# A layer norm's weights applied before the transpose, and products placed later by a planner

## The chip, the cores and the metric

The kernel runs on one core of a Trainium2 chip. The metric is the device time of one execution in microseconds (us). The engines of the core are TensorE (PE, matrix products; PEld is its loading of the stationary operand), VectorE (DVE), ScalarE (ACT), GpSimd (POOL) and SyncE (SP, which here issues nearly all transfers). They run side by side, each in the order in which its instructions were written, and wait for each other by semaphores.

## The reference

Two layers over 256 rows of 1,024 channels, then one more norm. A layer normalises its input, multiplies it by 9,808 columns of weights at once, lets three kinds of attention work on parts of the product, gates and merges their outputs, and adds the result to the input:

```
h = rms_norm(x, gain)                          # x * rsqrt(mean(x*x) + eps) * gain
proj = einsum('bsd,de->bse', h, w_in)
oa = moba_attention(rope(qa), rope(ka), va) * silu(ga)
ob = dsa_attention(rope(qb), rope(kb), vb, q_idx, k_idx, w_idx) * silu(gb)
log_f = log_sigmoid(f_logit + f_bias)
oc = forgetting_attention(qc, kc, vc, log_f) * silu(gc)    # logits + cumulative sums of log_f
y = einsum('nbsw,nwd->bsnd', stack([oa, ob, oc]), w_branch)
merged = sum(sigmoid(merge_logit) * y, over the three)
x = x + einsum('bsd,de->bse', merged, w_out)
```

After the second layer the rows are normalised with final_gain. Each attention has 8 heads of 64 columns.

## The kernel before

**Products in two parts.** All large products are made from float32 values split in two: a high part in the type fp32r and a low part, the rest. A weight comes from memory into one of three buffers called raw (1 MB each); ACT copies it into the high part wh (L381) and DVE subtracts to get the low part wl (L385). PE then adds three products: high by high, low by high and high by low. The normalised rows stand transposed as hTh and hTl. The sums grow in three banks called proj; d (two tiles of two banks) takes scores and transposes, and o (one bank) the attention's output.

**The order of work.** The program does not write its instructions as it states them. Each operation is put down with the tokens that it reads and writes, an estimated cost and a key (`plan.op`, L120). Then `Plan.run` (L150) goes through time: among the operations whose operands are there, it takes the engine that can start first, and on it the operation of the lowest key among those that can start then. The order that comes out is written to the engines, SP's queue of transfers included. An operation may carry a margin: the planner takes its operands to be there that much later than estimated. The estimate has no part in the run itself; where an operand comes later than planned, the engine waits with all that it has queued.

**Units.** A unit is one block of columns: `unit_a` (rows by 512 columns of weights, stationary the rows), `unit_b` (256 columns of weights stationary in two halves). Units are numbered as they are stated, and the number is the key of its matmuls; weight splits have a key 2 lower, their transfers 12 lower. A layer states, in this order, the first values (va), the index keys (kwf), the index scores and the MoBA mixer "a" mixed with gate units (m), the values and the mixer of "c" (forgetting attention), those of "b" (DSA), the rest of m and y, and the output product o.

**The norm** (`norm_to_hT`, L523) is made twice per layer, for each tile t of 128 rows: sums of squares of the two halves of 512 columns (L499 on ACT, L501 on DVE; in the second layer ACT alone), the mean (L505, DVE), the power -0.5 (L507, POOL), the rows times this factor (`scaled`: half 0 on ACT, L516, half 1 on DVE, L519), then eight transposes of 128 x 128 on PE (L537), and for each of the eight blocks a copy times the weight of the channel into hTh (L544, ACT) and a subtraction into hTl (L551, DVE). After the transpose a channel is a partition, so its weight is one scalar per partition, from the tile gT, which the host lays out as columns.

**The forget sums** (`wf_cols`, L783) make the forget gate's logarithms and their cumulative sums right after the index keys: exponential and logarithm on ACT (L802, L803; the logarithm needs another function table), nine small operations on DVE (L808 to L816), three products (L822 to L824), a transpose, and a way through memory into brow, which mixer c's biases read (L672).

**Attention** goes by pairs of heads: scores on PE (L613), maximum on DVE (L687), exponential on ACT (L691), normalising, transposes of the probabilities on PE (L624), split into pth (L716, ACT) and ptl (L717, DVE), and the values' products on PE (L729 to L732), of which L731 and L732 read ptl. Scores, transposes and values' products carry a margin of 200 ns (MARGIN).

**The opening.** SP sends the two halves of the first rows, the first weights, gT, and so on. PE runs 14 products of ones (L955) while nothing is there yet, and ten more (L1035, "warm") are planned at the lowest priority. `first_v` makes va of layer 0 in finer pieces: 48 matmuls of 512 columns (L1027).

**The last layer's end** sends final_gain, spread over the partitions, to acc (L1102) once the merged rows in acc have been read by the transposes L941; the output product adds to x (L1114), and the final norm follows.

Of the kernel before, what the change touches and what calls it, by code (L numbers as in the profile page):

```python
# [9 lines left out]
F32 = mybir.dt.float32  # L10
# [35 lines left out]
O_ORDER = ((0, (0, 1)), (1, (0, 1)), (0, (2, 3)), (1, (2, 3)))  # L46
M_ORDER = ((0, (0, 1)), (1, (0, 1)), (0, (2, 3)), (1, (2, 3)))
# [58 lines left out]
class Op:  # L106
    __slots__ = ("ways", "deps", "bufs", "new", "key", "n", "out", "need", "eng", "end", "lag", "name", "start",
                 "margin", "port", "banks")


class Plan:
# [8 lines left out]
    def op(self, ways, reads, writes, key, lag=0.0, name="", touch=()):  # L120
        o = Op()
        o.ways, o.key, o.lag, o.name, o.margin, o.port = ways, key, lag, name, 0.0, False
# [27 lines left out]
    def run(self, slack):  # L150
# [4 lines left out]
        while ready:  # L155
# [36 lines left out]
            e = min(best, key=best.get)  # L192
            lim = best[e] + slack.get(e, 0.0)
            t, _, _, o, w = min((c for c in cand if c[4][0] == e and c[0] <= lim), key=lambda c: (c[1], c[2]))
# [54 lines left out]
def hybrid_trunk(ctx, tc, x, norm_gain, w_in, forget_bias, w_branch, w_out, final_gain, consts, out):  # L249
# [51 lines left out]
    gT = pool.tile([128, L, KC], F32, name="gT")  # L301
# [29 lines left out]
    k_id, k_rope, k_gT, k_cst, k_fb, k_wf, k_widx, k_lf, k_cs, k_csT, k_main = (Tok() for _ in range(11))  # L331
# [179 lines left out]
    def scaled(i, src, t, reads, key):  # L511

        r = small[:, t, 3:4]
        o = tmp6[:, i * HD:(i + 1) * HD]
        if i == 0:
            act(lambda: ACT.activation(o, src, AF.Copy, scale=r), HD, False, reads + [k_ss[t][2]], [k_tmp[i]], key,  # L516
                "norm", 93.0)
        else:
            dve(lambda: DVE.tensor_scalar(o, src, r, None, op0=ALU.mult), HD, reads + [k_ss[t][2]], [k_tmp[i]], key,  # L519
                "norm", t_dve2(HD) + 61.0)  # L520
        return o

    def norm_to_hT(l, t, key):  # L523
        for i in range(2):
            sum_sq(t, i, key, l == 0)
        rstd(t, key)
        for i in range(2):
            scaled(i, xs[t][:, i * HD:(i + 1) * HD], t, [k_x[t][i]], key)
        dd = [Buf("d"), Buf("d")]
        for b in range(4):  # L530
            ps, at = Tok(), [dd[b // 2], dd[b // 2].banks[b % 2]]
            at_cols = lambda k, d=dd[b // 2], b=b: T(d)[:, b % 2 * 512 + k * 128:b % 2 * 512 + (k + 1) * 128]

            def tr(b=b, at_cols=at_cols):
                for k in range(2):
                    c = b * 2 + k
                    PE.transpose(at_cols(k), tmp6[:, c * 128:(c + 1) * 128], ident)  # L537
            pe(tr, 220.0, [k_tmp[b // 2], k_id], [ps], key, "hT", touch=at)
            for k in range(2):
                c = b * 2 + k  # L540
                sl = (slice(None), c, slice(t * 128, (t + 1) * 128))
                src = lambda at_cols=at_cols, k=k: at_cols(k)
                g = gT[:, l, c:c + 1]
                act(lambda sl=sl, src=src, g=g: ACT.activation(hTh[sl], src(), AF.Copy, scale=g), 128, True,  # L544
                    [ps, k_gT], [k_hT[0][t][c]], key, "hT", 93.0, touch=at)
            for k in range(2):
                c = b * 2 + k
                sl = (slice(None), c, slice(t * 128, (t + 1) * 128))
                src = lambda at_cols=at_cols, k=k: at_cols(k)
                g = gT[:, l, c:c + 1]  # L550
                dve(lambda sl=sl, src=src, g=g: DVE.scalar_tensor_tensor(  # L551
                    hTl[sl], src(), g, hTh[sl].bitcast(F32), op0=ALU.mult, op1=ALU.subtract), 128,
                    [ps, k_gT, k_hT[0][t][c]], [k_hT[1][t][c]], key, "hT", t_dve(128) + 61.0, touch=at)
# [520 lines left out]
    for l in range(L):  # L1074
# [15 lines left out]
        for f in between(first, m_of(l, 0, gates) + m_of(l, 2, gates, HC)):  # L1090
            f()
# [57 lines left out]
```

## Time and profile before

| What | Value |
|---|---|
| Median of 3 runs | 599.27 us (599.0 to 599.41) |
| The profiled execution | 598.98 us |
| Its span, first to last instruction | 597.1 us |
| TensorE's granted clock, mean | 0.999 |
| POOL busy | 100.2 us, 110 instructions |
| Bytes moved | 107.59 MB, mean 180 GB/s |

The profile is of one execution. A row of the timeline has the start and the duration in us, the engine, the line of the kernel, the operation, the tiles written and read, the shapes, how many like it follow each other, and, in brackets, how long the engine was idle before it and what ended that. Matmuls overlap, and their ends are modelled: a row of many shows a pitch, not a duration of one. The loading of a stationary operand (PEld) stands in rows of its own and runs ahead of the matmul. A row of waits has the total, the number and the longest. SP's waits are those of its queue of transfers.

### The profile page before, as it was taken

To read this page: it belongs to the slowest core of one execution; us is meant where nothing else is said; L and a number is where in the kernel's file an instruction comes from. 1 tells how busy PE (TensorE), PEld (TensorE's weight loads), DVE (VectorE), ACT (ScalarE), POOL (GpSimd) and SP (SyncE) were. 2 spreads that over 40 slices of the span, in tenths; PEclk is the share of its full clock that TensorE was granted. 3 is DMA by queue.
4 is the path that set the end of the run, shared out by engine and by line. 5 is a ranking of instruction groups with operands and counts; after the bars stand their busy time and mean duration, and the time that the engine had idled before them with its cause. 6 is when DMAs were issued, how large, how long until landed. Compare 5 with 4: busy or idle time off the path is not lost.

```text
span 597.1 us, 11359 instructions
## 1 busy us (share of the span) xinstructions
PE 587.2 (98%) x4332; PEld 538.2 (90%) x4332; DVE 516.8 (87%) x1164; ACT 387.0 (65%) x736; POOL 100.2 (17%) x110
## 2 busy tenths in 40 slices
PE   8999999999999999999999999999999999999995
PEld 7989998989998999888889899898999899998885
DVE  6799999877898989978588999997869898998773
ACT  5767539585677757774487754676748785758441
POOL 1241040200000334200004221320000023440001
PEclk9999999999999999999999999999999999999999
DMA  8849546546464554474546747464574464447411
GB/s 289 278 145 349 176 131 228 181 136 213 140 212 143 155 199 142 145 264 155 164 141 212 249 149 240 142 212 143 176 246 143 141 212 142 143 144 271 150 35 72
DMA packets 75831, 107.59 MB, mean 180 GB/s; under 512 B 4208, under 2 KB 45440, under 8 KB 75776
## 3 DMA queue, kind: packets, MB, share of 16 engines
q1 hardware_dynamic: 75488, 106.47, 54.4%
q8 instruction: 34, 0.56, 0.4%
q10 hardware_dynamic: 288, 0.39, 0.2%
q14 instruction: 21, 0.17, 0.1%
HBM read 105.79 MB, written 1.06 MB: 179 GB/s over the span
## 4 chain that ended last, share of the span: by engine, by line
PE 85%; DVE 10%; issue 2%; ACT 1%; DMA 1%; POOL 0%; POOLq 0%; DVEq 0%
PE proj L429 74%; PE d L613 4%; DVE wl L385 3%; PE proj L1027 2%; PE d L624 2%; PE o L732 1%; PE o L729 1%; DVE isc L891 1%; DVE t L890 1%; PE o L731 1%; PE d L941 1%; DVE rsh L488 1%; DMA x<-in_x_dram 1%; PE o L730 0%; ACT wh L381 0%
## 5 line engine op out<-in xcount | busy, mean ns | idle before, releaser
L385 DVE TENSOR_TENSOR wl<-raw,wh 128x1024 fp32r<-128x1024 f32 (+1 forms) x190 | 235.1, 1250 | 26.3 <-ACT wh L381 23.2
L381 ACT ACTIVATE wh<-raw 128x1024 fp32r<-128x1024 f32 (+1 forms) x190 | 198.2, 1055 | 74.7 <-PE proj L429 37.1
L429 PE MATMUL proj<-hTh,wh 128*128 128x256 f32 (+1 forms) x656 | 155.6, 276 | 0.0
L429 PE MATMUL proj<-hTl,wh 128*128 128x256 f32 (+1 forms) x656 | 154.9, 275 | 0.0
L429 PEld LDWEIGHTS proj<-hTh,wh 128*128 128x128 f32 (+1 forms) x656 | 125.2, 191 | 0.6
L429 PEld LDWEIGHTS proj<-hTl,wh 128*128 128x128 f32 (+1 forms) x656 | 125.2, 191 | 0.3
L429 PE MATMUL proj<-wh,hTh 128*128 128x512 f32 x272 | 105.1, 386 | 0.0
L429 PE MATMUL proj<-wh,hTl 128*128 128x512 f32 x272 | 103.3, 380 | 0.2 <-DVE hTl L551 0.2
L429 PE MATMUL proj<-hTh,wl 128*128 128x256 f32 (+1 forms) x656 | 100.4, 276 | 0.0
L429 PEld LDWEIGHTS proj<-hTh,wl 128*128 128x128 f32 (+1 forms) x656 | 86.2, 191 | 0.2
L429 PE MATMUL proj<-wl,hTh 128*128 128x512 f32 x272 | 81.0, 379 | 0.3 <-DVE wl L385 0.3
L489 POOL TENSOR_TENSOR rsh<-rsh,cst 128x256 f32<-128x256 f32 (+1 forms) x42 | 38.4, 915 | 165.9 <-DVE rsh L488 164.3
L429 PEld LDWEIGHTS proj<-wl,hTh 128*128 128x128 f32 x272 | 51.3, 189 | 7.9 <-DVE wl L385 0.7
L429 PEld LDWEIGHTS proj<-wh,hTl 128*128 128x128 f32 x272 | 51.5, 189 | 7.5 <-DVE hTl L551 1.2
L429 PEld LDWEIGHTS proj<-wh,hTh 128*128 128x128 f32 x272 | 51.4, 189 | 7.5
L691 ACT ACTIVATE e<-e,st 128x128 f32<-128x128 f32 x96 | 42.4, 443 | 22.8 <-DVE st L687 22.5
L491 POOL TENSOR_TENSOR rr<-rr,rsh 128x256 f32<-128x256 f32 (+1 forms) x42 | 41.5, 989 | 12.6 <-DVE rr L490 8.8
L752 POOL TENSOR_TENSOR ot<-ot,g 128x256 f32<-128x256 f32 x10 | 8.1, 814 | 200.6 <-DVE ot L747 129.1
L429 PE MATMUL proj<-wh,v 128*128 128x512 f32 (+1 forms) x144 | 34.0, 359 | 0.0
L429 PEld LDWEIGHTS proj<-wh,v 128*128 128x128 f32 x144 | 25.1, 190 | 2.8
L429 PE MATMUL proj<-wh,og0h 128*128 128x512 f32 x64 | 25.0, 391 | 0.0
L717 DVE TENSOR_TENSOR ptl<-d,pth 128x768 fp32r<-128x768 f32 x24 | 22.9, 953 | 2.2 <-ACT pth L716 1.9
(193 smaller groups left out, 926.8 us busy)
## 6 DMA issues: line engine op xcount, KB each, us to landing
raw<-in_w_in_dram SPq DMA_DIRECT2D x74, 1024.0 KB, 5.2
raw<-in_w_branch_dram SPq DMA_DIRECT2D x12, 1024.0 KB, 5.1
raw<-in_w_out_dram SPq DMA_DIRECT2D x8, 1024.0 KB, 5.1
brow<-drow SPq DMA_DIRECT2D x4, 512.0 KB, 6.6
raw<-in_w_in_dram SPq DMA_DIRECT2D x3, 512.0 KB, 6.2
x<-in_x_dram SPq DMA_DIRECT2D x4, 256.0 KB, 5.5
raw<-in_w_in_dram SPq DMA_DIRECT2D x2, 320.0 KB, 6.2
out_dram<-tmp SPq DMA_DIRECT2D x2, 320.0 KB, 2.5
```

The lines of the kernel that those rows point to most:

```text
L381: ACT.activation(p[0].v, sel(c.v), AF.Copy)
L385: DVE.tensor_tensor(p[1].v, sel(c.v), p[0].v.bitcast(F32), op=ALU.subtract)
L429: PE.matmul(o(), a(), b(), start=first and i == 0, stop=last and i == n - 1)
L488: dve(lambda: DVE.stream_shuffle(T(sh)[:np_], a(), SWAP), S, [ps], [sh], key, "rope", t_dve(S) + 6.0)
L489: gps(lambda: POOL.tensor_tensor(T(sh)[:np_], T(sh)[:np_], s[:np_], op=ALU.mult), S, [k_rope], [sh], key, "rope")
L491: gps(lambda: POOL.tensor_tensor(T(r)[:np_], T(r)[:np_], T(sh)[:np_], op=ALU.add), S, [sh], [r], key, "rope")
L613: PE.matmul(T(d)[:, c:c + n].rearrange("p (b a) -> p b a", a=2), st[r, sl], turns(mv[r, :n]), start=i == 0, stop=i == 2, skip_group_check= ...
L624: PE.matmul(T(d)[:, u * 512 + j * 64:u * 512 + j * 64 + 64], e[r], ident[r, r], is_transpose=True, start=True, stop=True, skip_group_check ...
L691: act(lambda t=t, a=a, n=n, e=e, st=st: ACT.activation(T(e)[:, a:a + n], T(e)[:, a:a + n], AF.Exp, bias=T(st)[:, t:t + 1], scale=-1.0, acc ...
L717: dve(lambda src=src, dst=dst: DVE.tensor_tensor(dst(pl), src(), dst(ph).bitcast(F32), op=ALU.subtract), 128 * n, [ps, k[0]], k[1:], key, ...
L752: plan.op([("POOL", t_pool(S), lambda: POOL.tensor_tensor(*gate(), op=ALU.mult)), ("DVE", t_dve(S), lambda: DVE.tensor_tensor(*gate(), op= ...
L1027: PE.matmul(T(ps[t]).rearrange("p (b a) -> p b a", a=2), h(2 * i + x, t), turns(v3(w)[:, x]), start=left[t][0] == 23, stop=left[t][0] == 0)
```

## The change

- **The norm.** The weights multiply the rows before the transpose, where a channel is a column. So they are needed as a row, the same on all partitions. For layer 0 the row (4 KB) is the first transfer of all, into a part of brow; two products of a single row of ones with 512 columns of it spread it over the partitions into a tile of d (gain0, held until both tiles of rows have been normed). For layer 1 the row is sent spread to acc, as the final gain was, before the output product's units of layer 0. One DVE instruction per half (rows times factor times weights) takes the place of `scaled`. gT and the host's layout for it go.
- **512 wide.** Per half: four transposes, one copy to hTh, one subtraction to hTl (before: eight blocks of 128, two by two). A tile of rows uses one tile of d instead of two. Sums of squares may go to either engine in both layers.
- **Rush.** Operations of the norm that only DVE or POOL can do may be taken up to 400 ns ahead of their start by the planner, so that the engine is kept for them. In layer 1 the norm's keys are the unit's less 10 and 8 (before: less 2).
- **Margins.** Scores and transposes of the probabilities 300 ns, values' products 600 ns (before: 200 for all).
- **The forget sums** get the key of the unit after mixer a instead of the index keys'; only the part that reads the product's result from the bank stays.
- **The opening.** Each tile of rows is one transfer, not two halves; the memset of half comes after the first loads; one early Tanh on ACT.

```diff
+RUSH = 400.0
+NK = (10, 8)
...
-            e = min(best, key=best.get)
+            e = min(cand, key=lambda c: c[0] - c[3].rush)[4][0]
             lim = best[e] + slack.get(e, 0.0)
-            t, _, _, o, w = min((c for c in cand if c[4][0] == e and c[0] <= lim), key=lambda c: (c[1], c[2]))
+            t, _, _, o, w = min((c for c in cand if c[4][0] == e and c[0] <= lim + c[3].rush), key=lambda c: (c[1], c[2]))
...
     def norm_to_hT(l, t, key):
+        a = len(plan.ops)
         for i in range(2):
-            sum_sq(t, i, key, l == 0)
-        rstd(t, key)
+            sum_sq(t, i, key, True)
+        r = rstd(t, key)
+        d = Buf("d")
         for i in range(2):
...
+            c = slice(i * HD, (i + 1) * HD)
+            x, o = xs[t][:, c], tmp6[:, c]
+            g = (lambda c=c: T(gain0)[:, c]) if l == 0 else (lambda c=c: acc[:, 0, c])
+            rg, tg = ([k_gain], [gain0]) if l == 0 else ([k_fg, k_acc[0][0], k_acc[1][0]], [])
+            dve(lambda x=x, o=o, g=g: DVE.scalar_tensor_tensor(o, x, r, g(), op0=ALU.mult, op1=ALU.mult), HD,
+                [k_x[t][i], k_ss[t][2]] + rg, [k_tmp[i]], key, "norm", touch=tg)
+            at, kt, ks4 = [d, d.banks[i]], Tok(), slice(4 * i, 4 * i + 4)
+
+            def tr(i=i, o=o, d=d):
+                for j in range(4):
+                    PE.transpose(T(d)[:, i * 512 + j * 128:i * 512 + (j + 1) * 128], o[:, j * 128:(j + 1) * 128], ident)
+            pe(tr, 480.0, [k_tmp[i], k_id], [kt], key, "hT", touch=at)
+            src = lambda i=i, d=d: T(d)[:, i * 512:(i + 1) * 512].rearrange("p (k s) -> p k s", k=4)
+            h, lo = (x[:, ks4, t * 128:(t + 1) * 128] for x in (hTh, hTl))
+            act(lambda h=h, src=src: ACT.activation(h, src(), AF.Copy), HD, True, [kt], k_hT[0][t][ks4], key, "hT", touch=at)
+            dve(lambda h=h, lo=lo, src=src: DVE.tensor_tensor(lo, src(), h.bitcast(F32), op=ALU.subtract), HD,
+                [kt] + k_hT[0][t][ks4], k_hT[1][t][ks4], key, "hT", t_dve(HD) + 10.0, touch=at)
+        for o in plan.ops[a:]:
+            if {w[0] for w in o.ways} <= {"DVE", "POOL"}:
+                o.rush = RUSH
...
-        pe(go, sum(cost) + SWITCH, [r for x in reads for r in x], [w for x in writes for w in x], key, name, MARGIN,
+        pe(go, sum(cost) + SWITCH, [r for x in reads for r in x], [w for x in writes for w in x], key, name, 300.0,
...
-            pe(av, 696.0, kv + [ph, pl] + [t for h in kp for t in h], [o], key, "av", MARGIN)
+            pe(av, 696.0, kv + [ph, pl] + [t for h in kp for t in h], [o], key, "av", 600.0)
...
-    for i in range(2):
-        load(xs[0][:, i * HD:(i + 1) * HD], xr[0][:, i * HD:(i + 1) * HD], 512 * HD, [k_x[0][i]], -102 + i, "x0", 950.0)
-    load(gT.rearrange("p l k -> p (l k)"), norm_gain, 8192, [k_gT], -94.9, "gain")
+    load(brow[:1, :4].rearrange("p h c -> p (h c)"), norm_gain[:1], 4096, [k_grow] + k_row[:4], -103, "gain", 950.0)
+    load(xs[0], xr[0], 512 * D, k_x[0], -102, "x0", 950.0)
+    DVE.memset(half, -0.5)
+    ACT.activation(csum[:, 0, :1], half, AF.Tanh)
+    gain0 = Buf("d")
+
+    def gain_rows():
+        for i in range(2):
+            PE.matmul(T(gain0)[:, i * HD:(i + 1) * HD], ones[:1], brow[:1, 2 * i:2 * i + 2].rearrange("p h c -> p (h c)"),
+                      start=True, stop=True)
+    pe(gain_rows, 1800.0, [k_grow] + k_row[:4], [k_gain], -99, "gain", touch=[gain0])
...
-        wf_cols(l, u + 1)
+        sums = wf_cols(l, u + 1)
...
+        sums(units[0])
         v_units(l, "c", 1)
...
-        if last:
-            dma(lambda: nc.sync.dma_start(acc[:, 0],
-                                          final_gain.rearrange("(o d) -> o d", o=1).to_broadcast([128, D])),
-                512 * D, [], [k_fg] + [t for k in k_acc for t in k], units[0], "final gain")
+        g = final_gain.rearrange("(o d) -> o d", o=1) if last else norm_gain[l + 1:l + 2]
+        dma(lambda g=g: nc.sync.dma_start(acc[:, 0], g.to_broadcast([128, D])), 512 * D, [],
+            [k_fg] + [t for k in k_acc for t in k], units[0], "next gain")
...
-                    norm_to_hT(l + 1, t, u - 2)
+                    norm_to_hT(l + 1, t, u - NK[t])
```

More of the change, by code (lines that the diff above doesn't have):

```diff
@@ L107 @@
     __slots__ = ("ways", "deps", "bufs", "new", "key", "n", "out", "need", "eng", "end", "lag", "name", "start",
-                 "margin", "port", "banks")
+                 "margin", "port", "banks", "rush")
 class Plan:
@@ L121, in op @@
         o = Op()
-        o.ways, o.key, o.lag, o.name, o.margin, o.port = ways, key, lag, name, 0.0, False
+        o.ways, o.key, o.lag, o.name, o.margin, o.port, o.rush = ways, key, lag, name, 0.0, False, 0.0
         deps, o.bufs = {}, []
@@ L300, in hybrid_trunk @@
     qs = [[pool.tile([128, S], F32R, name=f"q{p}{i}") for i in range(3)] for p in "hl"]
-    gT = pool.tile([128, L, KC], F32, name="gT")
     hTh = pool.tile([128, KC, S], F32R, name="hTh")
@@ L329, in hybrid_trunk @@
     widx = pool.tile([128, 2, 8], F32, name="widx")
-    k_id, k_rope, k_gT, k_cst, k_fb, k_wf, k_widx, k_lf, k_cs, k_csT, k_main = (Tok() for _ in range(11))
+    k_id, k_rope, k_grow, k_gain, k_cst, k_fb, k_wf, k_widx, k_lf, k_cs, k_csT, k_main = (Tok() for _ in range(12))
     k_row = [Tok() for _ in range(8)]
@@ L509, in rstd @@
         return small[:, t, 3:4]
[L511 to L521, printed above, removed]
@@ L523, in norm_to_hT @@
     def norm_to_hT(l, t, key):
+        a = len(plan.ops)
         for i in range(2):
-            sum_sq(t, i, key, l == 0)
-        rstd(t, key)
+            sum_sq(t, i, key, True)
+        r = rstd(t, key)
+        d = Buf("d")
         for i in range(2):
[L528 to L553, printed above, removed]
@@ L799, in wf_cols, with forget @@
         dve(pre, 0, [ps, k_fb], [k_lf], key, "lf", 300.0)
+        return lambda k: forget(l, k, z, na, e, u, c, lf)
+    def forget(l, key, z, na, e, u, c, lf):
         def ln():
@@ L951, in hybrid_trunk @@
     DVE.memset(ones, 1.0)
-    DVE.memset(half, -0.5)
     warm, spare = plan.tags["d"][0][1], plan.tags["o"][0][1]
@@ L973, in late_loads @@
     def late_loads():
-        for i in range(2):
-            load(xs[1][:, i * HD:(i + 1) * HD], xr[1][:, i * HD:(i + 1) * HD], 512 * HD, [k_x[1][i]], -90 + i, "x1")
+        load(xs[1], xr[1], 512 * D, k_x[1], -90, "x1")
         load(cst[:, C_ROPE:], consts[:, C_ROPE:], 512 * 1024, [k_rope], -12 + 1.5, "rope")
@@ L1136 @@
     feed = {n: np.ascontiguousarray(inputs[n]) for n in _INS}
-    feed["norm_gain"] = np.ascontiguousarray(feed["norm_gain"].reshape(L * KC, 128).T)
     feed["consts"] = shape_constants()
```

## The prediction

> **What bounds the kernel now.** I read the page first, then the busy time by stretches, then what TensorE's weight loads waited for, then the timeline at the places that these name. From the page, the span and the engines:
>
> ```profile
> span 597.1 us, 11359 instructions
> ...
> PE 587.2 (98%) x4332; PEld 538.2 (90%) x4332; DVE 516.8 (87%) x1164; ACT 387.0 (65%) x736; POOL 100.2 (17%) x110
> ```
>
> TensorE (PE) is the bound: it is busy almost everywhere, and the change takes no matmul of the layers away. All that can be won is time in which PE stands. The stretches (span, then busy time and count of PE, PEld, DVE, ACT, POOL; clock; DMA share; GB/s) say where that is:
>
> ```profile
> 0.00:12.00 12.00, 10.51 (x60) 9.44 (x60) 6.78 (x22) 6.61 (x16) 1.25 (x7) 1.00 0.83 282
> ...
> 57.00:70.00 13.00, 13.00 (x85) 12.03 (x84) 13.00 (x31) 6.38 (x9) 2.52 (x4) 1.00 0.50 163
> ...
> 85.00:95.00 10.00, 9.77 (x72) 8.26 (x72) 10.00 (x37) 6.23 (x22) 2.64 (x3) 1.00 0.33 107
> 95.00:105.00 10.00, 9.04 (x91) 8.67 (x86) 9.96 (x15) 9.11 (x14) 0.00 (x0) 1.00 0.88 285
> ...
> 285.00:312.00 27.00, 26.80 (x131) 22.86 (x130) 18.11 (x35) 16.82 (x36) 1.10 (x2) 1.00 0.50 164
> ...
> 350.00:380.00 30.00, 30.00 (x216) 27.80 (x215) 30.00 (x83) 14.15 (x18) 5.79 (x8) 1.00 0.54 177
> 380.00:395.00 15.00, 14.49 (x117) 13.02 (x116) 14.79 (x43) 13.26 (x30) 1.36 (x1) 1.00 0.55 179
> ```
>
> PE idles 1.2 us in 85 to 105 (20.00 less 9.77 and 9.04), 0.5 in 380 to 395, 0.2 at the layer boundary. In the same stretches, and ahead of them, VectorE (DVE) is busy without a break: there it is a second bound, and PE's idle time is DVE's lateness. What the weight loads waited for (total, times, longest; PEld runs ahead of the matmul and sees a stall first):
>
> ```profile
> PEld o L731 <- DVE ptl L717: 1.9, 4, 1.1
> PEld proj L429 <- DVE hTl L551: 1.2, 3, 0.6
> ...
> PEld proj L429 <- DVE wl L385: 0.7, 1, 0.7
> PEld d L624 <- DVE fb L672: 0.7, 2, 0.3
> PEld d L613 <- DVE k2l L416: 0.4, 1, 0.4
> ...
> PEld d L624 <- DVE e L701: 0.3, 1, 0.3
> ```
>
> These 5.2 us, and the opening, are all that the change can reach.
>
> **The values' products (margin 200 to 600 ns).** The planner writes PE's order from estimated times. A product whose operand is late in fact holds everything that PE has behind it, and with that the engines that read its results. The row "o <- ptl" has four such holds, 1.9 us, the longest 1.1 and so 0.8 for the other three. With 400 ns more of margin the planner places other matmuls ahead, and each hold shrinks by up to 0.4: 0.4 of the longest and the 0.8, 1.2 us. At best 1.9; at worst nothing, where the matmul that comes first instead meets a late wl of the same full DVE.
>
> **Scores and transposes (margin 200 to 300).** The rows of L613 and L624 hold 1.4 us in five waits; 0.1 for each is 0.5. Ends: 0 and 1.4.
>
> **The layer boundary.** For each tile of rows the chain becomes, twice: a 512-wide product with the weights on DVE, four transposes, one ScalarE (ACT) copy, one DVE subtraction. Before:
>
> ```profile
> 297.41 0.55 POOL L507 TENSOR_TENSOR small<-small,half 128x1 f32<-128x1 f32 x1 [37.49 <-DVE small L505]
> ...
> 297.99 0.49 DVE L519 TENSOR_SCALAR tmp<-x,small 128x512 f32<-128x512 f32 x1 [0.66 <-POOL small L507]
> 298.00 0.72 ACT L516 ACTIVATE tmp<-x,small 128x512 f32<-128x512 f32 x1
> ...
> 298.40 3.26 DVE L385 TENSOR_TENSOR wl<-raw,wh 128x1024 fp32r<-128x1024 f32 x3
> ...
> 300.20 2.15 ACT L544 ACTIVATE hTh<-d,gT 128x128 fp32r<-128x128 f32 x8
> ...
> 302.43 1.89 DVE L551 SCALAR_TENSOR_TENSOR hTl<-d,gT,hTh 128x128 fp32r<-128x128 f32 x7
> ```
>
> The merged rows are already copied and subtracted 512 wide, and price the new instructions:
>
> ```profile
> 284.19 0.58 ACT L946 ACTIVATE v<-d 128x512 fp32r<-128x512 f32 x1
> ...
> 285.45 0.68 DVE L947 SCALAR_TENSOR_TENSOR v<-d,v 128x512 fp32r<-128x512 f32 x1
> ```
>
> ACT: 0.72 + 2.15 = 2.87 becomes 2 x 0.58 = 1.16 per tile. DVE: 0.49 + 8 x 0.27 (1.89 / 7) = 2.65 becomes 4 x 0.68 = 2.72, so nothing is won on the fuller engine. What is won is latency. From 298.0 the two products end at 299.4; with 0.2 us for each handoff (an estimate: at the start half of eight transposes end near 7.35, and their copy begins at 7.50, rows below) the second four transposes (0.55) end near 300.1, the copy near 300.9, the last hTl near 301.8. Before it was 302.43 + 1.89 = 304.3, with three splits of 3.26 us let ahead; the earlier keys and the rush of 400 ns turn that order round. So the 1.2 us of hTl waits go; the matmuls, which lag PEld, lose less, and I take 0.6 (ends 0 and 1.2). The cover: the three splits come 2 to 3 us later, and with them the release of the raw buffers. Their matmuls begin some 2.6 us (12 at 6.48 / 30 = 0.216, row below) after the first, so nothing; 0.3 if that is short.
>
> **The weights' transfer in layer 0.** The last layer has the like of it, and SyncE's (SP) queue waits there for acc:
>
> ```profile
> SPq L1102 <- DVE acc L932: 7.8, 1, 7.8
> ```
>
> ```profile
> 283.08 18.97 SPq L373 DMA_DIRECT2D raw<-in_w_in_dram  x5
> ...
> 283.40 0.60 PE L941 MATMUL d<-cst,acc 128*128 128x128 f32 x4
> ```
>
> In layer 0 the next weight load, at 283.08, queues behind it, and acc is free only when L941 is done, at 284.0: that load leaves 1 to 1.5 us later. Its pieces are for matmuls after 300. Nothing; 0.5 if the ring is tighter.
>
> **The forget sums, put later.**
>
> ```profile
> 29.96 1.28 ACT L803 ACT_TABLE_LOAD   x1
> 31.25 0.22 ACT L803 ACTIVATE fz<-fz 128x16 f32<-128x16 f32 x1
> ```
>
> ```profile
> L808 DVE TENSOR_SCALAR fz<-fz x2: 151/392/632, 34.8 to 323.1; 128x16 f32<-128x16 f32 x2
> ...
> L816 DVE SCALAR_TENSOR_TENSOR fz<-fz x2: 174/174/175, 37.1 to 325.6; 128x16 f32<-128x16 f32 x2
> ```
>
> Nine small DVE operations, 34.8 to 37.3, 2.5 us, leave the place just ahead of the wl that PE waits 0.7 for, and land in a later gap of the same engine. I take -0.4 and +0.4: nothing. Ends: -1.2 (they pass the full stretch, and PE's idle time in 85 to 105 goes) and +3.2 (rival below). On ACT each table switch is 1.28 by the row, and the next activation starts 1.29 after the load does; two of them per layer now fall among softmax's exponentials, where ACT is busy 6.23 of 10 and has 3.77 free: 2.6 fits. The Trainium skill (ScalarE: Activation LUTs, What ACT_TABLE_LOAD costs) counts about 2.66 us for a switch, 1.38 of it a drain; by that the two would take 5.3, 1.5 more than is free, and the sum below would be -0.5 instead of -2.0. This trace shows the load and no drain behind it.
>
> **The opening.**
>
> ```profile
> 1.05 5.64 PE L955 MATMUL d<-ones 128*128 128x128 f32 x28 [1.05 <-DVE half L952]
> ...
> 5.44 0.55 POOL L507 TENSOR_TENSOR small<-small,half 128x1 f32<-128x1 f32 x1 [4.14 <-DVE small L505]
> ...
> 6.80 1.09 PE L537 MATMUL d<-cst,tmp 128*128 128x128 f32 x8
> ...
> 7.50 0.89 ACT L544 ACTIVATE hTh<-d,gT 128x128 fp32r<-128x128 f32 x3 [0.23 <-PE d L537]
> 7.92 0.48 PE L1027 MATMUL proj<-wh,hTh 128*128 128x512 f32 x1
> 9.93 2.17 PE L1035 MATMUL o<-ones 128*128 128x128 f32 x18
> ...
> 11.29 1.08 ACT L1016 ACTIVATE wh<-raw 128x1024 fp32r<-128x1024 f32 x1
> ```
>
> and from the chain of waits:
>
> ```profile
> 16.15 6.48 PE proj L1027 x30
> ```
>
> The 48 first matmuls (10.4 us) and 16 transposes (2.2) could end 12.6 us after 6.80; they end at 22.63. Some 3.2 us are lost, because ACT and DVE are at hT until the split at 11.29. The narrower chain frees them sooner. But the gain's two products stand on PE behind the 28 warm-up records, which end at 6.7. One such product (one row, 512 columns, plain fp32) is not in the trace; the warm-up's, 128 wide, take 5.64 / 14 = 0.40 with the slow start, 2.17 / 9 = 0.24 later, so four times that: 0.96 to 1.6. PE is warm by then; I take 0.96. They end at 8.6, while the factor is ready at 5.99. The first normed half so starts at 7.9 (if DVE waits for its own half alone) or 8.8, and the first matmul comes 0.68 + 0.2 + 0.55 + 0.2 + 0.58 + 0.2 later: 10.3 or 11.2, not 7.92. With 10.4 and the other 12 transposes (1.6) the stretch ends at 22.3 or 23.2. On DVE the splits of the first weights queue behind the two products, which may hold the hTl matmuls another 0.9. I take 0; ends -1.0 and +1.5. The single transfer of x and the early table load act on what is now waiting for the gain anyway.
>
> **Sum:** -1.2 - 0.5 - 0.6 + 0 + 0 + 0, and +0.3 for holds that a new order brings: -2.0. The profiled execution took 598.98 (1.88 around the span), 0.29 under the median of 599.27; on the median the forecast is 597.3.
>
> **Rivals.** (1) The holds move: DVE's load is the same, so PE's idle time in 85 to 105 and 380 to 395 stays under other names, and only the boundary's 0.6 is won: 598.7. For it: 13.00 of 13.00 and 30.00 of 30.00. Against: four holds at one instruction, L731. (2) Slower: the forget sums land inside the full stretch. DVE has no gap there, so their 2.5 us come out at its end, less the 0.5 won ahead: +2.0 in layer 0; in layer 1, where PE idles less, half as much, +1.2; and the values' 1.2 is lost again: 597.3 + 3.2 + 1.2 = 601.7. It decides once more than 2 us of DVE's work pass into that stretch. Against: before it DVE is nearly as full. (3) The sums pass beyond 105 and the opening gains: -1.2 - 0.5 more: 595.6. (4) ACT is held by the switches for longer than their row says: at twice 1.28 each, 5.1 per layer against 3.77 free, softmax is 1.3 us later: 598.6. Against: 31.25 follows 29.96 at once. That the change does not do what it says is the late gain in the opening, in its ends above.
>
> **Chances:** forecast 0.46, (1) 0.22, (2) 0.14, (3) 0.13, (4) 0.05. About 0.2% (1.2 us) is what a measurement can tell here. Faster by more: 0.42 of the first, all of (3), 0.05 of (1): 0.60; slower 0.14, from (2); the same 0.26. The range, 595.4 to 600.8, takes in (3), (1), (4) and the milder half of (2).
>
> **What would show it.** Right: the wait of L731 for ptl under 0.8 us; no hTl wait at the boundary, the last hTl of the first tile near 302; the first proj matmul after 10, yet the opening's end near 22.6. Wrong: DVE rows of fz between 57 and 105 with PE idle behind them; PE idle over 1.7 us in all of 57 to 105 and 380 to 395; first matmul before 9 or the opening ending after 24.

## The result and the profile after

The changed kernel takes 604.27 us (median of 4 runs, 603.63 to 605.54), the kernel before beside it 599.34. The ratio is 1.0085 (95% interval 1.0066 to 1.0104): 4.9 us slower, where 2.0 faster was forecast. The profiled execution is the slowest of the four, 605.54 us. Its page:

```profile
span 603.7 us, 11316 instructions
...
PE 591.4 (98%) x4336; PEld 541.7 (90%) x4336; DVE 522.6 (87%) x1154; ACT 377.8 (63%) x706; POOL 91.9 (15%) x103
```

PE's busy time grew by 4.2 us for 4 more records. The four are the two spreading products, 1.98 us; for the rest, the same products took longer somewhere. The stretches of the kernel after (columns as before: span, busy time and count of PE, PEld, DVE, ACT, POOL, then the clock, which is the share of its full speed that PE was granted, DMA share, GB/s):

```profile
0.00:12.00 12.00, 9.78 (x40) 7.94 (x40) 3.64 (x9) 3.60 (x7) 1.26 (x7) 0.91 0.81 287
8.00:9.00 1.00, 0.86 (x3) 0.03 (x1) 0.01 (x1) 0.00 (x0) 0.00 (x0) 1.00 0.97 385
9.00:10.00 1.00, 0.21 (x1) 0.21 (x2) 1.00 (x2) 0.00 (x0) 0.00 (x0) 0.88 1.04 406
10.00:11.00 1.00, 1.00 (x6) 1.00 (x6) 1.00 (x3) 0.00 (x0) 0.00 (x0) 0.50 1.06 410
14.00:17.00 3.00, 3.00 (x12) 2.58 (x11) 2.46 (x4) 2.86 (x6) 0.82 (x1) 0.57 0.19 55
17.00:20.00 3.00, 3.00 (x22) 2.79 (x21) 2.54 (x3) 0.00 (x0) 0.12 (x1) 1.00 0.96 295
...
95.00:105.00 10.00, 9.23 (x72) 7.90 (x71) 10.00 (x27) 9.20 (x21) 1.49 (x2) 1.00 0.46 150
...
380.00:395.00 15.00, 13.94 (x104) 12.05 (x103) 15.00 (x42) 11.51 (x28) 3.63 (x4) 1.00 0.45 144
```

In the first 12 us PE does 40 records instead of 60, and the clock is 0.91 instead of 1.00. From 10 to 17 it is at half: 12 records in the 3 us from 14, and 22 in the next three. Where DVE is full, PE stands 0.77 us in 95 to 105 and 1.06 in 380 to 395: 1.83 in all, where it was 1.70. What the weight loads wait for:

```profile
PEld d L529 <- DVE tmp L523: 3.0, 3, 1.8
...
PEld d L609 <- DVE e L686: 1.5, 3, 0.8
PEld proj L1022 <- DVE wl L1014: 1.3, 1, 1.3
PEld d L598 <- DVE k3l L417: 1.3, 1, 1.3
PEld proj L1022 <- ACT hTh L533: 1.1, 1, 1.1
...
PEld proj L430 <- DVE hTl L534: 0.6, 2, 0.3
PEld o L716 <- DVE ptl L702: 0.5, 2, 0.3
```

The values' products wait 0.5 us for ptl, where it was 1.9: that part did what it should. Transposes and scores wait longer for DVE than before (L609 and L598 here 1.5 and 1.3 us; L624 and L613 had 1.4 together). The rows of L529 and L1022 had 0.3 us or nothing before, and most of their time lies in the opening. Its timeline:

```profile
1.05 5.90 PE L943 MATMUL d<-ones 128*128 128x128 f32 x28 [1.05 <-DVE half L953]
...
5.68 0.56 POOL L508 TENSOR_TENSOR small<-small,half 128x1 f32<-128x1 f32 x1 [4.37 <-DVE small L506]
...
6.88 1.98 PE L959 MATMUL d<-brow,ones 1*128 1x512 f32 x4
...
8.99 1.41 DVE L523 SCALAR_TENSOR_TENSOR tmp<-x,small,d 128x512 f32<-128x512 f32 x2 [3.40 <-PE d L959]
9.79 1.97 PE L529 MATMUL d<-cst,tmp 128*128 128x128 f32 x8 [0.93 <-DVE tmp L523]
...
11.79 0.60 ACT L533 ACTIVATE hTh<-d 128x512 fp32r<-128x512 f32 x1 [4.21 <-PE d L529]
12.43 0.69 DVE L534 TENSOR_TENSOR hTl<-d,hTh 128x512 fp32r<-128x512 f32 x1 [0.83 <-ACT hTh L533]
12.45 1.22 PE L1022 MATMUL proj<-wh,hTh 128*128 128x512 f32 x2 [0.69 <-ACT hTh L533]
13.15 0.60 ACT L533 ACTIVATE hTh<-d 128x512 fp32r<-128x512 f32 x1 [0.76 <-DVE hTl L534]
```

Read the brackets. The factor is ready at 6.24, but DVE stands until both spreading products are done (8.99). ACT's first copy stands until all eight transposes are done (11.79), not its own four. The second copy stands for the first hTl. And two products of 512 columns take 1.22 us at 12.45, and eight transposes 1.97 at 9.79, where eight took 1.09 in the kernel before (at 6.80). That is the clock: in the kernel before it is granted in full from 5.8 on, here it is full from 6.35 to 9.76 and half from 9.76 to 16.59.

The loss is followed best by one and the same matmul. Both kernels have 3,336 matmuls that write proj; the table gives how much later than in the kernel before the n-th of them starts (us, profiled executions; "norm 1" is layer 1's norm, at the layer boundary). A minus is earlier.

| Kernel | 1st (7.92) | 48th (22.24, opening's end) | 1,650th (299.17, ahead of norm 1) | 1,700th (312.48, behind it) | last (590.73) |
|---|---|---|---|---|---|
| after | +4.53 | +6.49 | +5.94 | +6.57 | +6.53 |
| old opening | +0.11 | +0.11 | -0.80 | -0.14 | -0.20 |
| new opening only | +4.35 | +5.07 | +5.56 | +5.57 | +5.55 |
| spread over 128 rows | +3.64 | +4.15 | +3.59 | +4.23 | +4.18 |
| dummies behind | +4.50 | +5.01 | +4.44 | +5.09 | +5.03 |
| no weights | +0.71 | +1.22 | +0.65 | +1.30 | +1.27 |
| no weights, a tile each | +0.41 | -0.78 | -1.34 | -0.69 | -0.72 |
| after, a tile each | +3.75 | +5.23 | +4.51 | +5.16 | +5.13 |
| by transfer | +1.32 | +1.85 | +1.14 | +1.79 | +1.73 |
| by transfer, a tile each | +0.59 | +0.03 | -0.71 | -1.42 | -1.44 |
| norm 1 only | -0.11 | -0.11 | +0.43 | +1.08 | +1.03 |
| norm 1 only, a tile each | -0.19 | -0.18 | +0.29 | -0.42 | -0.48 |

In the kernel after, the whole loss is there at the 48th matmul. Behind that the parts of the change win and lose again (the 200th comes 5.01 us later, the 700th 6.16), and little of it is left at the end.

### The profile page after: what moved, and what is told of

Read it like the earlier page. It is cut to its first block, busy times and chain, and to the rows that moved or that the text cites. A ratio compares the mean times of both kernels' runs of the same rounds, so it can differ in the third digit from the quotient of the medians.

```text
span 603.7 us, 11316 instructions
## 1 busy us (share of the span) xinstructions
PE 591.4 (98%) x4336; PEld 541.7 (90%) x4336; DVE 522.6 (87%) x1154; ACT 377.8 (63%) x706; POOL 91.9 (15%) x103
## 3 DMA queue, kind: packets, MB, share of 16 engines
HBM read 106.31 MB, written 1.06 MB: 178 GB/s over the span
## 4 chain that ended last, share of the span: by engine, by line
PE 83%; DVE 14%; issue 2%; ACT 1%; POOL 0%; POOLq 0%; DVEq 0%
PE proj L430 70%; DVE wl L386 5%; PE d L598 3%; PE d L609 2%; PE proj L1022 2%; DVE isc L880 1%; PE d L943 1%; PE o L717 1%; PE o L714 1%; DVE rsh L489 1%; PE d L529 1%; DVE t L879 1%; DVE isc L858 1%; DVE rr L491 1%; PE d L930 1%
## 5 line engine op out<-in xcount | busy, mean ns | idle before, releaser
L386 DVE TENSOR_TENSOR wl<-raw,wh 128x1024 fp32r<-128x1024 f32 (+1 forms) x190 | 237.9, 1265 | 24.8 <-ACT wh L382 23.5
L490 POOL TENSOR_TENSOR rsh<-rsh,cst 128x256 f32<-128x256 f32 (+1 forms) x42 | 34.4, 818 | 230.5 <-DVE rsh L489 230.4
L492 POOL TENSOR_TENSOR rr<-rr,rsh 128x256 f32<-128x256 f32 (+1 forms) x42 | 44.5, 1061 | 6.0 <-DVE fz L797 1.6
L701 ACT ACTIVATE pth<-d 128x768 fp32r<-128x768 f32 x24 | 19.4, 809 | 9.0 <-PE d L609 5.2
```

The costliest lines, as they stand in the source:

```text
L386: DVE.tensor_tensor(p[1].v, sel(c.v), p[0].v.bitcast(F32), op=ALU.subtract)
L490: gps(lambda: POOL.tensor_tensor(T(sh)[:np_], T(sh)[:np_], s[:np_], op=ALU.mult), S, [k_rope], [sh], key, "rope")
L492: gps(lambda: POOL.tensor_tensor(T(r)[:np_], T(r)[:np_], T(sh)[:np_], op=ALU.add), S, [sh], [r], key, "rope")
L701: act(lambda src=src, dst=dst: ACT.activation(dst(ph), src(), AF.Copy), 128 * n, True, [ps], k[:1], key, "pT", touch=[ph] + ps.banks)
```

## The experiments

My theory after this reading: the loss is the opening, and in it (A) the clock falls because PE works on products of a single row, (B) the norm waits for those products, and (C) the new chain itself is no faster. The rivals: the loss is spread over the rest of the kernel; the clock falls because PE stands idle behind the products, not because of their form; the forget sums in the full DVE stretch cost it. Each time is a median with the ratio to the kernel before run beside it (599.34 to 599.6).

**The old opening in the kernel after** (layer 0's norm, gT and the first transfers as in the kernel before; all else as after).

```
-        norm_to_hT(0, t, -50 + t)
+        norm_old(0, t, -50 + t)
```

> The changed kernel with the opening of before (weights of layer 0 after the transpose, gT, two halves of x, no products that spread a row); layer 1's norm, margins, rush and forget sums as changed. Theory A (all of the loss is in the opening, where the 48th matmul comes 6.5 us later): about 604.3 - 6.5 = 597.8 us, the 48th matmul of the layers near 22.2. Rival B (the planner's new order of the layers costs, and the opening's delay would have been absorbed in the full VectorE stretch): 601 or more.

598.70 us, ratio 0.9985 (0.9976 to 0.9995). Theory A had 597.8, but took its 6.5 us from the profiled execution, the slowest of four; rival B had 601 or more. The rest of the change is worth 0.8 us to the good. The loss is the opening, and the rival that spreads it falls.

**The new opening alone in the kernel before** (margins, sums and layer 1 as before).

```
-        norm_to_hT(0, t, -50 + t)
+        norm_new(0, t, -50 + t)
```

> The kernel before with the opening of the kernel after alone (weights by two one-row products, halves 512 wide, x in one transfer); the margins, the sums' places and layer 1 stay as before. Theory: the opening is the whole loss, so the 48th matmul comes 6 to 7 us behind, as in the kernel after, and the time is 604.7 to 606.2: as much slower as the kernel after, and 0.5 to 1.5 more, since the margins' gain is missing. Rival: the loss in the opening needs the sums' removal or the early rush as well; then it is less than 4 us and the time under 603.5.

604.77 us, ratio 1.0090 (1.0076 to 1.0104), in its theory's range, though the 48th matmul is 5.07 behind and not 6 to 7: 5.3 us lost by the opening with nothing else, not even the planner's rush. That is the other half of the proof.

**The spreading products over 128 rows** (127 of them zero, so that the result is the same).

```
+    DVE.memset(brow[:, :4].rearrange("p h c -> p (h c)"), 0.0)
...
-            PE.matmul(T(gain0)[:, i * HD:(i + 1) * HD], ones[:1], brow[:1, 2 * i:2 * i + 2].rearrange("p h c -> p (h c)"),
+            PE.matmul(T(gain0)[:, i * HD:(i + 1) * HD], ones, brow[:, 2 * i:2 * i + 2].rearrange("p h c -> p (h c)"),
```

> The two products that spread the weights use all 128 rows of the array (row 0 the weights, 127 rows of zeros, ones as stationary), same columns and same length. Theory A1 (the clock falls to half at 9.8 because the products occupy one row of the array): the clock stays full, about 3 us won, 601.3. Rival A2 (it falls because TensorE stands from 8.9 to 9.8 and after): no change, 603.5 to 604.5, half clock from about 9.8 to 16.6 as before.

603.22 us, ratio 1.0061 (1.0044 to 1.0078): 1.05 less than the kernel after, where theory A1 had 3, but with the full clock that it asked for. Its timeline, and the same stretches:

```profile
6.74 1.88 PE L960 MATMUL d<-brow,ones 128*128 128x512 f32 x4
9.55 1.31 PE L529 MATMUL d<-cst,tmp 128*128 128x128 f32 x8 [0.93 <-DVE tmp L523]
```

```profile
8.00:9.00 1.00, 0.62 (x2) 0.00 (x0) 0.25 (x1) 0.34 (x1) 0.00 (x0) 1.00 1.05 408
9.00:10.00 1.00, 0.45 (x4) 0.42 (x4) 1.00 (x2) 0.00 (x0) 0.00 (x0) 1.00 1.01 401
10.00:11.00 1.00, 0.86 (x6) 0.42 (x4) 1.00 (x3) 0.10 (x1) 0.00 (x0) 1.00 1.02 399
11.00:12.00 1.00, 0.45 (x2) 0.42 (x3) 0.82 (x2) 0.50 (x1) 0.00 (x0) 1.00 1.06 412
```

The products take as long as those of one row (1.88 and 1.98 us), PE stands 0.93 us behind them in both runs, and yet here the clock stays full. The 3.41 us ahead of the fall in the kernel after:

```profile
6.35:9.76 3.41, 2.51 (x9) 1.07 (x8) 0.77 (x2) 0.63 (x1) 0.00 (x0) 1.00 1.01 383
```

and the like stretch of this run:

```profile
6.24:9.65 3.41, 2.48 (x11) 1.17 (x11) 1.39 (x5) 1.50 (x4) 0.55 (x1) 1.00 0.94 288
```

PE is busy for 2.51 and 2.48 us, with the same products in the same order. So it is the single row that costs the clock. At the 48th matmul this is worth 2.3 us (6.49 less 4.15), in the medians 1.05. The two differ because the four executions of the kernel after are of two kinds: two have a mean clock of 0.991 (605.54, the profiled one, and 604.80 us), two of 0.994 (603.63 and 603.74 us). With 128 rows all four have 0.999.

**Four products of ones behind the two** (PE's idle time in 8.9 to 9.8 is filled).

```
+        for _ in range(4):
+            PE.matmul(spare[:, :128], ones, ones, start=True, stop=True)
```

> Four products of ones stand behind the two that spread the weights and fill the 0.9 us until the first transposes. Theory A1 (one row of the array is too little activity for the whole window): no change, 603.5 to 604.5, since the window still holds 1.9 us of them. Rival A2 (standing is what lowers the clock): the clock stays full, about 601.3.

604.92 us, ratio 1.0091 (1.0074 to 1.0108), 0.4 above its theory's range. The clock falls all the same, from 8.6 to 12.0, although PE was busy without a break in the 3.41 us ahead:

```profile
5.14:8.55 3.41, 3.41 (x18) 2.04 (x18) 0.29 (x2) 1.21 (x3) 0.55 (x1) 1.00 0.94 297
8.55:11.96 3.41, 3.17 (x16) 2.77 (x14) 2.47 (x4) 0.20 (x1) 0.00 (x0) 0.50 1.05 410
```

The idle time is not the cause of the fall. In this profiled execution (604.03 us, mean clock 0.995) it lasts half as long as in the kernel after, and the 48th matmul is at +5.01. Two of the four executions have 0.992, and take 605.77 and 606.05 us.

**No weights in layer 0** (a tile of ones in their place, without transfer and products; this leaves layer 0's norm weights out of the result).

```
+    POOL.memset(acc[:, 0], 1.0)
...
-    pe(gain_rows, 1800.0, [k_grow] + k_row[:4], [k_gain], -99, "gain", touch=[gain0])
```

> Layer 0's weights are left out: a tile of ones, set by GpSimd, stands in their place, and there are no products and no transfer for them; everything else as changed. Theory A (the wait for the weights behind the warm-up, and the slow clock that follows it, are the loss): the first norm starts near 6.3, the first matmul near 9.3, the clock stays full, 597 to 598.5. Rival C (the chain itself, 512 wide and with both halves waiting for each other, is what costs): the first matmul near 9.3, but the 48th still 2 us or more later than before's, 600.5 or more.

600.42 us, ratio 1.0015 (1.0005 to 1.0024), next to rival C's 600.5. Clock and wait are gone, and at the 48th matmul 1.22 us remain. So the wait for the products is 2.9 (4.15 less 1.22; the same stands at the first matmul, 3.64 less 0.71), and the chain itself is slower than the old one. Where, its ACT rows and one of PE show:

```profile
7.97 0.60 ACT L533 ACTIVATE hTh<-d 128x512 fp32r<-128x512 f32 x1 [0.74 <-PE d L529]
9.33 0.60 ACT L533 ACTIVATE hTh<-d 128x512 fp32r<-128x512 f32 x1 [0.76 <-DVE hTl L534]
9.82 1.05 ACT L1004 ACTIVATE wh<-raw 128x1024 fp32r<-128x1024 f32 x1
...
19.68 0.70 PE L1015 MATMUL proj<-wl,hTh 128*128 128x512 f32 x2 [0.88 <-DVE wl L1007]
```

ACT has the same two waits for the other half as in the kernel after, and behind them a split of weights comes late for PE. The diff has a line that could make them: the kernel before gave each half a tile of d of its own, the change puts both into one.

**The same with a tile of d for each half in layer 0** (layer 0's weights left out here too).

```
-        d = Buf("d")
+        dd = [Buf("d"), Buf("d")] if l == 0 else [Buf("d")] * 2
         for i in range(2):
+            d = dd[i]
```

> The kernel after without layer 0's weights (as in the run that left them out: 600.42 us, 48th matmul 1.22 us behind the kernel before), and with a PSUM tile of its own for each half's transposes in layer 0, instead of the two halves of one tile. It leaves out layer 0's norm weights. In that run the first copy hTh started 7.97, after all eight transposes, and the second copy stood 0.76 for the first hTl. Theory: the wait for the other half comes from the shared tile. Then the first copy starts about 0.6 us earlier (four transposes instead of eight), the second no longer waits for the first hTl, the 48th matmul comes 0.5 to 1.2 us earlier than there, and the time is 599.2 to 600.0. Rival: the waits are for the engines and for the tiles of the split input, not for that tile; then the copy's start and the 0.76 us stay, and the time is 600.3 to 600.5.

598.24 us, ratio 0.9980 (0.9971 to 0.9989), 1.0 below its theory's range. The same ACT rows:

```profile
7.70 1.07 ACT L534 ACTIVATE hTh<-d 128x512 fp32r<-128x512 f32 x2
8.65 1.06 ACT L1005 ACTIVATE wh<-raw 128x1024 fp32r<-128x1024 f32 x1
```

Both copies go back to back, the split behind them starts 1.2 us earlier, and PE's wait of 0.88 us for wl is gone. The shared tile costs 2.0 us at the 48th matmul (1.22 against -0.78). Without it, and with no weights to wait for, the new opening ends 0.8 us ahead of the old one. Theory C, that the chain as such is no faster, falls: it was the tile. With the weights there, sent by a transfer, the lead is used up (+0.03, "by transfer, a tile each").

**The kernel after with a tile each in layer 0**, the products kept (same edit).

> The kernel after, with a PSUM tile of its own for each half's transposes in layer 0; the two one-row products stay. Theory (loss at the 48th matmul: clock 2.3, wait for the products 2.9, shared tile 1.2 to 2.0): 48th matmul 4.3 to 5.3 us behind the kernel before, half clock for one or two windows as in the kernel after, time 602.2 to 603.2. Rival: the shared tile costs only where the chain is short, and behind the late products it is hidden by them; then the 48th stays 6 or more behind and the time is 604 or more.

603.49 us, ratio 1.0066 (1.0050 to 1.0081). 1.26 us at the 48th matmul and 0.8 in the medians; the time lies 0.3 above the theory's range. It does not come to 2.0 because the planner now sends the second half's transposes later, at 13.95 instead of behind the first four at 10.07, and the clock is still half. It has no choice: d has two tiles, gain0 holds one of them, and so both halves use the other in turn (its last reader, the first half's hTl, ends at 12.48). The run does not show what two tiles at the same time would be worth beside the products.

**The weights by a transfer** (layer 0's weights spread by a transfer of 512 KB into the accumulator's free half; no products).

```
-    load(brow[:1, :4].rearrange("p h c -> p (h c)"), norm_gain[:1], 4096, [k_grow] + k_row[:4], -103, "gain", 950.0)
+    load(acc[:, 0], norm_gain[:1].to_broadcast([128, D]), 512 * D, [k_gain], -101, "gain", 950.0)
```

> The kernel after, but layer 0's weights come to all 128 rows by a transfer of 512 KB into the accumulator's free half, queued behind the first rows of x, and the two products are gone. Theory (the loss is 2.3 us of clock and 2.9 of waiting for the products): both go if the transfer lands before 6; with the chain's own 1.2 us left, the 48th matmul comes some 1.2 to 1.6 us behind the kernel before, no window of half clock behind 6, and the time is 600.2 to 600.9. Rival: 512 KB more in the stretch where the DMA engines are full delay the first weights by as much as they take, 1.3 us at 400 GB/s, or the gain lands as late as the products ended; then the 48th comes 2.5 to 4 us behind and the time is 601.5 to 603.

600.70 us, ratio 1.0020 (1.0011 to 1.0029), as its theory had it. From 7.18 on the clock is full and stays so. DVE stands until the weights land, at 6.42, 2.6 us before the products' 8.99:

```profile
6.42 1.41 DVE L523 SCALAR_TENSOR_TENSOR tmp<-x,small,acc 128x512 f32<-128x512 f32 x2 [0.94 <-DMA acc<-in_norm_gain_dram]
```

**The layer boundary: the new norm in layer 1 only** (row in acc, 512 wide, rush, the earlier keys; one tile of d, as in the change).

```
-                    norm_to_hT(l + 1, t, u - 2)
+                    norm_to_hT(l + 1, t, u - NK[t])
```

> The kernel before with only layer 1's norm changed (weights as a row in acc, 512 wide, rush, earlier keys). Theory A: the boundary's waits go, 0.6 us less, 598.9. Rival F (TensorE stands for the second tile's products of rows and weights, as the changed kernel's profile has it at 311, so the boundary costs): 0.3 to 0.8 us more, 599.8 to 600.3.

600.21 us, ratio 1.0010 (1.0001 to 1.0019): 0.6 us slower, with the lower end of the interval barely above 1, where the prediction had -0.6; it is the time that rival F asked for. And with a tile of d for each half (the edit shown above, here in layer 1):

> The kernel before with layer 1's norm in the new form (as in the run of that alone: 600.21 us, and 0.65 us lost between the 1650th and the 1700th matmul), and with a PSUM tile of its own for each half's transposes. Theory: as in layer 0, where tiles of their own gave back 2.0 us, the copies that wait for the other half are the loss; then the boundary falls from +0.65 to 0 or below, and the time is 598.9 to 599.6. Rival: the loss is the wait of the second tile's transposes for the second product on DVE (1.3 us in two waits), which no PSUM tile changes; then +0.4 to +0.7 stays, and the time is 599.9 to 600.4.

598.92 us, ratio 0.9989 (0.9980 to 0.9998). From the 1,650th to the 1,700th matmul the one loses 0.65 us, the other wins 0.71. The first tile's rows with one tile of d:

```profile
298.41 1.42 DVE L568 SCALAR_TENSOR_TENSOR tmp<-x,small,acc 128x512 f32<-128x512 f32 x2 [0.67 <-POOL small L509]
...
300.88 0.60 ACT L578 ACTIVATE hTh<-d 128x512 fp32r<-128x512 f32 x1 [0.56 <-PE d L574]
301.52 0.69 DVE L579 TENSOR_TENSOR hTl<-d,hTh 128x512 fp32r<-128x512 f32 x1 [0.56 <-ACT hTh L578]
302.24 0.60 ACT L578 ACTIVATE hTh<-d 128x512 fp32r<-128x512 f32 x1 [0.76 <-DVE hTl L579]
302.74 0.62 ACT L501 ACTIVATE tmp<-x 128x512 f32<-128x512 f32 x1
302.87 0.69 DVE L579 TENSOR_TENSOR hTl<-d,hTh 128x512 fp32r<-128x512 f32 x1 [0.66 <-ACT hTh L578]
...
306.83 1.32 PE L574 MATMUL d<-cst,tmp 128*128 128x128 f32 x8 [0.63 <-DVE tmp L568]
```

and with a tile each:

```profile
298.27 1.42 DVE L569 SCALAR_TENSOR_TENSOR tmp<-x,small,acc 128x512 f32<-128x512 f32 x2 [0.67 <-POOL small L509]
...
300.31 1.08 ACT L579 ACTIVATE hTh<-d 128x512 fp32r<-128x512 f32 x2
300.94 1.29 DVE L580 TENSOR_TENSOR hTl<-d,hTh 128x512 fp32r<-128x512 f32 x2
301.28 0.63 ACT L501 ACTIVATE tmp<-x 128x512 f32<-128x512 f32 x1
...
305.73 1.09 PE L575 MATMUL d<-cst,tmp 128*128 128x128 f32 x8
```

The first tile's last hTl ends at 302.23 instead of 303.56, the sums of squares of the second tile follow at 301.28 instead of 302.74, and the second tile's transposes no longer stand in PE's queue waiting for their operand (0.63 us on PE). The rival, that this wait has nothing to do with the tile, falls.

**The margins alone in the kernel before**, both, and then the values' alone.

```
-            pe(av, 696.0, kv + [ph, pl] + [t for h in kp for t in h], [o], key, "av", MARGIN)
+            pe(av, 696.0, kv + [ph, pl] + [t for h in kp for t in h], [o], key, "av", 600.0)
```

> The kernel before with only the margins changed (scores and transposes 300 ns, values' products 600 ns). Theory A (the values' holds are TensorE's to win, as the prediction had it): 1.2 to 1.7 us less, 597.9 to 598.4 against 599.5, and the wait of the values' products for ptl under 0.8 us. Rival D (another product meets the same full VectorE instead): 599.2 to 599.8, with the wait for ptl smaller and other waits larger by as much.

> The kernel before with the margin of the values' products alone, 200 to 600 ns; scores and transposes keep theirs. Both margins together gave 598.05 us against 599.57. The prediction's shares: 1.2 us from the values', 0.5 from the others. By these it is 598.1 to 598.5. Rival: the two share the same holds, and the gain comes from scores and transposes moving, not from the values'; then 599.0 to 599.5.

598.05 us, ratio 0.9976 (0.9967 to 0.9985), and 598.15, ratio 0.9977 (0.9968 to 0.9985). The whole gain is the values'; scores and transposes add nothing that is measured. With the values' margin alone the holds at L731 are down from four and 1.9 us to

```profile
PEld o L731 <- DVE ptl L717: 0.7, 1, 0.7
```

**The forget sums alone**, and with the margins.

```
-        wf_cols(l, u + 1)
+        sums = wf_cols(l, u + 1)
...
+        sums(units[0])
```

> The kernel before with only the forget sums put later. The changed kernel's curve fell 1.5 us behind its opening's delay while the index scores run, and this is the part of the change that acts there. Theory E (the sums leave the way of the index stage and fill gaps later): 0.8 to 1.4 us less, 598.1 to 598.7. Rival D (given back in the full VectorE stretch from 57 to 105): 599.2 to 599.8.

> The kernel before with the margins and the later forget sums, and neither new norm. If the boundary costs (F) and the sums win (E), this is the fastest kernel here: 597.6 to 598.4, below the one that keeps before's opening alone (598.7). If the boundary wins (A): slower than that one, 599.0 or more.

599.34 us, ratio 0.9998 (0.9989 to 1.0007), and 598.19, ratio 0.9979 (0.9970 to 0.9989). The sums alone put the 200th matmul (46.06) 1.27 us ahead, and by the 700th it is all given back (+0.04). The prediction had this null as -0.4 and +0.4; a gain and a loss came, three times as large, and theory E of the run, which had the gain alone, falls.

**What the new form is worth when its two faults are gone.** The kernel after by transfer and with a tile each in both layers; and the kernel after with the old opening and a tile each in layer 1.

> The kernel after with layer 0's weights spread by a transfer instead of products (that alone: 600.70 us) and a PSUM tile of its own for each half in both layers. It computes what the reference does. Theory: the transfer run's +1.85 at the 48th matmul loses the 2.0 us of the shared tile and comes to about 0; with what the margins give, 598.4 to 599.0; if the boundary gains too, 597.8 to 598.4. Rival: the transfer of 512 KB is itself late (factor and weights wait for it), so the 48th stays 1 us or more behind and the time is 599.5 or more.

> The kernel after with the opening of the kernel before (that alone: 598.7 us) and a PSUM tile of its own for each half in layer 1: margins, sums' places and the new form in layer 1, without the new form in layer 0. Theory: the boundary's 0.65 us goes with the shared tile; then 597.7 to 598.2, as good as or better than the margins alone (598.05 to 598.15). Rival: the wait for the second product stays; then 598.5 to 598.8.

597.65 us, ratio 0.9969 (0.9957 to 0.9980), and 597.37, ratio 0.9965 (0.9953 to 0.9978). Both beat the kernel before and the kernel after, and come out where the prediction had put the change (597.3), each a little below its theory's range. Their intervals overlap, and that of the margins alone overlaps both.

## Why the prediction was wrong

By parts, with the differences to the kernel before run beside each:

| Part | Forecast | Measured |
|---|---|---|
| Values' products | -1.2 | -1.3 |
| Scores and transposes | -0.5 | -0.2 (-1.5 for both margins) |
| Layer boundary | -0.6 | +0.6 |
| Forget sums | 0 | -0.2 |
| Opening | 0 (ends -1.0 and +1.5) | +5.3 |
| All | -2.0 (with +0.3 for new holds) | +4.9 |

The single parts add to 4.2; the 0.7 that is missing is about what the intervals leave open.

- **The opening is the step that failed**: "I take 0; ends -1.0 and +1.5". It cost 5.3. The working started the first matmul at 10.3 or 11.2 and let 48 products and 12 transposes follow without a gap, 12.0 us. In the kernel after the first comes at 12.45 and the stretch to the 48th's end takes 16.7; in the kernel before it took 14.7, and without weights and with a tile each, the shortest of the runs with the new form in layer 0, 13.5. Three costs were left out or taken as paid: the wait, the clock and the shared tile.
- **Which operand DVE waits for** was left open there (7.9 or 8.8). It is both halves: 8.99. The run without the weights and the one over 128 rows put this wait at 2.9 us (2.8 in the medians, 603.22 less 600.42), the largest of the three. The prediction had seen it, and then let it vanish in "The narrower chain frees them sooner": it reckoned that the lost time of the old opening, 3.2 us, would pay for a first matmul that comes 2.4 to 3.3 us later. What the new form pays back is at most 1.2: without weights and with a tile each, the first matmul comes 0.4 later and the opening ends 0.8 earlier.
- **The clock.** "PE is warm by then; I take 0.96" was right for the duration: the two products take 1.98 us. But the working had no term for what they do to the clock behind them: two windows of 3.41 us at half rate in the profiled execution, and none in the run over 128 rows. The upper end that was costed (1.6 for each product) was a slow product, not a slow PE for 6.8 us afterwards.
- **The shared tile** was in the diff and even in its description (one tile of d instead of two), and no step priced it. The handoff of 0.2 us, read where each half had a tile, was carried over to a chain where it has not. Measured: 2.0 us in layer 0, and in layer 1 the difference between +0.65 and -0.71. With a tile each the boundary's -0.6 holds and its last hTl ends at 302.23, forecast 301.8.
- **The values' margin** was right in size and place: each hold shrinks by what the planner moves it. The scores' share was too large; the lines quoted for it hold four waits, not five, and in the kernel after other waits of the same two operations stand in their place (1.5 and 1.3 us).
- **The forget sums** and the rival that feared them: their DVE rows came at 43.85 to 46.07 and at 332.4 to 335.2, ahead of the full stretches, and the slower case of 601.7 did not arise. ACT's function-table switch in the kernel after:

```profile
37.20 0.20 ACT L791 ACTIVATE fz<-fz 128x16 f32<-128x16 f32 x1
37.41 1.28 ACT L792 ACT_TABLE_LOAD   x1
38.71 0.21 ACT L792 ACTIVATE fz<-fz 128x16 f32<-128x16 f32 x1
```

  The load starts 0.01 us after the activation ahead of it ends, and the next activation starts 1.30 after the load does. The Trainium skill (ScalarE: Activation LUTs, What ACT_TABLE_LOAD costs) counts about 2.66 us, a drain included; this trace shows no room for the drain ahead of the load or behind it, and the row was the better price.
- **The case of the other sign** was put into the wrong place. The only rival slower than before lay in the forget sums; the opening, where the change adds an operation that no row of the trace showed, had ends of -1.0 and +1.5. Its sign for the opening did name the failure: it ended at 29.1, "after 24". The sign by PE's idle time from 57 to 105 and 380 to 395, "over 1.7", tells little: it was 1.70 before and is 1.83, and as the kernel after runs 6.5 us late, these stretches hold other work there (380 to 395 has 1.06 us of idle time, 386.5 to 401.5 none).

## What to carry to other kernels

An operation that the trace does not show can cost more through what it does to its engine than through its own duration, so a bound that only stretches its duration is no bound. When a change puts two halves into one tile, look up who waits for whom afterwards: a copy may then wait for the other half's producers and readers, and a handoff time read off separate tiles no longer holds. And at the opening of a kernel ask which operand arrives last on the one chain that everything waits for: here the rows' factor stood ready 2.6 us before the weights that were to be multiplied along with it.

## What the runs showed of the hardware

Two products of one row by 512 columns, on a PE that the profile calls busy, were followed by 3.41 or 6.83 us at half clock in all four runs that had them (after, the new opening alone, the dummies, the tile each), and by none in any run without them or with 128 rows. Over single executions, the mean clock is 0.991 to 0.995 in all 16 of these four kernels and 0.996 to 0.999 in all of the others. The full part between warm-up and fall was 3.41 us long each time. The Trainium skill (TensorE: Matmul & The Clock Gate, What's actually happening) describes a free-running window of 3,413 ns over which activity is judged, with half rate until a busy window has passed; the lengths here agree with that. What exactly is counted within a window these runs do not settle. PE's busy time in the profile does not decide the fall: with 3.41 us of 3.41 the clock fell (dummies), with 2.48 it stayed (128 rows). Behind the fall, stretches of 3.41 us at half clock with PE busy for 2.48 to 2.72 us (after, the new opening alone, the tile each) were followed by another at half, and those with 3.17 or more by full clock.

That a copy waits for the transposes of the other half is an effect of how the tiles' users are tracked, as far as these runs show: the two halves lay in different banks of d in both forms, and only the tile's identity was changed.
